# Sixteen more tokens by row gather, routing by four heads, and a second-table sum that grows in the tile of the normalized tokens

## The chip, the cores and the metric

The kernel runs on one core of a Trainium2 chip. The metric is the device time of one execution in microseconds (us), lower is better; differences of over about 0.3% can be told from no change.

## The reference

A decoder block for 512 tokens of width 2048, all in float32: an RMS norm, one input projection to 10240 columns, a gated short convolution and a stick-breaking attention side by side, their gated merge, an output projection with the residual, and then an expert network (PEER). The change lies in the last part:

```python
def peer_ffn(x, wq, subkeys, u_table, v_table):
    q = jnp.einsum("btd,dq->btq", x, wq).reshape(b, t, PEER_HEADS, 2, PEER_HALF)
    scores = jnp.einsum("bthsc,snc->bthsn", q, subkeys)
    top_s, top_i = lax.top_k(scores, PEER_TOPK)
    cand_s = top_s[..., 0, :, None] + top_s[..., 1, None, :]
    cand_i = top_i[..., 0, :, None] * PEER_KEYS + top_i[..., 1, None, :]
    sel_s, sel_pos = lax.top_k(cand_s.reshape(...), PEER_TOPK)
    sel_i = jnp.take_along_axis(cand_i, sel_pos, axis=-1)
    gate = jax.nn.softmax(sel_s, axis=-1)
    # of each token: 8 heads x 16 experts, out of 16384
    hidden = jnp.einsum("td,thkd->thk", xb, u_table[idx])
    act = jax.nn.gelu(hidden, approximate=False) * gate
    return jnp.einsum("thk,thkd->td", act, v_table[idx])
```

The result is added to the residual and normalized once more (norm_final).

## The kernel before, in words

**Two ways to the experts.** The first `G0` tokens (128 + 64 = 192) fetch the rows of the two tables that they chose, by indirect DMA from the POOL queue. The other `ND` = 320 tokens go through all 16384 experts on TensorE ("dense"): `up` multiplies them with every block of 128 rows of the first table, `gates` builds planes that hold each token's gate or zero, and `products` multiplies the gated activations with the second table. The gathers run in the background of everything that comes after the routing of the first tokens.

**Products.** Each weight half tile (128 x 1024) is loaded by SP, rounded to fp32r by ScalarE (`whi`, L133), and VectorE takes the remainder (`wlo`, L134). Each product is then three matmuls (`mm3`, L163: lines L164, L165, L166) of 128 x 128 weights by the columns of the tokens: 256 columns in the mixer's and the queries' projections, 320 (all `ND` tokens) in `up` (tile `pj`) and in `products` (tile `z`). Up and down have 2048 products each.

**Routing** (`route`, L549) works on a tile of 128 tokens, all 8 heads at once: top 16 of each of 16 score groups, the 64 possible sums of two lists, their top 16, the positions' decoding (small operations on [128, 8, 16]), one-hot sums for the expert numbers, the gates. The order of this side work is written out: `background` (L956) is called once for each half weight tile and lets the routing go on for a share of its own cost marks (`yield 2.0` and so on); `pump` (L906) lets the gather go on by RATE rounds for each unit (a whole weight tile). In the dense part the rate is worked out so that all rounds are done some ten units before the end.

**Gather** (`gather_tile`, L676): one round fetches one row of 2048 for each of 128 partitions (1 MB, L685) into one of four buffers `row`. For the first table VectorE multiplies it with the normalized tokens `gx` and sums (L696); for the second it adds the row times its activation to `acc` (L703), which is itself one of the four `row` buffers, loaded with the residual at its start. Tokens 0 to 127 take 128 rounds of each table. The next 64 tokens lie twice on the partitions, each copy with half of the slots, so 64 rounds of each table; `finish` adds the two halves and the norm and the store follow (`finish_rows`, L722; its sum of squares by `rms_scale`, L189, goes through two PSUM tiles `z`).

**The end.** Before the last chunk's `down` the rest of the gather is let run ("last", L919). The residual of the dense tokens is loaded into the same `row` buffers (L882). As each of eight pairs of column blocks is done, TensorE transposes it back in three groups of tokens (`tr`, L843), VectorE adds it to the residual (L845), ScalarE takes squares (L847), VectorE multiplies the gain (L848). The last three rows are scaled and stored.

The program is put in order by a scheduler with a simulated time line, engine by engine; each engine runs its list in that order.

Of the kernel before, what the change touches and what calls it, by code (L numbers as in the profile page):

```python
# [25 lines left out]
H = 8  # L26
# [5 lines left out]
NG2 = 64  # L32
# [48 lines left out]
def block_kernel(ctx, tc, a, out, dbg=None):  # L81
# [107 lines left out]
    def rms_scale(pool, x):  # L189
        ss = pool.tile([P, 2], F32, name="ss", bufs=2)  # L190
        for c in range(2):
            junk = ztile()
            nc.scalar.activation(junk, x[:, c * 1024:c * 1024 + 1024], AF.Square, accum_out=ss[:, c:c + 1])  # L193
        return rms_inv(ss)

    def rms_inv(ss):
        nc.vector.tensor_tensor(ss[:, 0:1], ss[:, 0:1], ss[:, 1:2], OP.add)
        nc.scalar.activation(ss[:, 0:1], ss[:, 0:1], AF.Sqrt, scale=1.0 / D, bias=epst)
# [3 lines left out]
    def turn(x2, k, pin):  # L202
        """Two 128-column blocks of the pair of row tiles, transposed: [128, 2, 256]."""
# [9 lines left out]
    def load_x(h):  # L213
        """Transposed tokens of one half times the norm's gains, split; 1 / rms of each token to inv."""
# [206 lines left out]
    def suffix(pool, z, sp, seg, nj, W):  # L421
        """z minus the sums of sp over the keys from each key to the end."""
# [22 lines left out]
    def outproj(pool, h, m, box):  # L445
        """Output projection and residual of 256 tokens."""
# [38 lines left out]
    def chain(pool, h, box, nhi, nlo, c0):  # L485
        """Normalized, transposed and split tokens of one half from column c0; tokens 0.. to xn2d."""
# [35 lines left out]
    def queries(pool, h, st, nhi, nlo, c0):  # L522
        """Product-key scores of 256 tokens, queued for the top 16 of each group."""
# [25 lines left out]
    def route(pool, tile_no, st):  # L549
        """Product-key routing of one 128-token tile: expert halves and gate of each slot."""  # L550
        ls = pool.tile([P, 2, 8, 2, 16], F32, name="ls", bufs=1)
        tv, ti = ls[:, 0], ls[:, 1].bitcast(U32)
        for _ in range(8):
            while not st["topk"][tile_no]:
                yield "wait"
            for _ in range(2):
                src, g = st["topk"][tile_no].pop(0)
                tmp = pool.tile([P, P], F32, name="ttmp", bufs=2)
                top16(tmp, src, tv[:, g // 2, g % 2], ti[:, g // 2, g % 2])
            yield 2.0  # L560
        tif = pool.tile([P, 8, 2, 16], F32, name="tif", bufs=1)
# [166 lines left out]
    def gather(routes):  # L728
# [6 lines left out]
        if not NG2:  # L735
            return
# [351 lines left out]
```

## Time and profile before

| | us |
|---|---|
| median of 3 runs | 3630.6 |
| the three runs | 3629.32, 3630.6, 3640.37 |
| profiled execution, span | 3629.1 |

The profiled execution is known by its span, first instruction to last, 3629.1 us; it is 1.5 us under the median of the runs. TensorE is busy 3535.7 us of it (97%), VectorE 2833.4 (78%), ScalarE 1621.6 (45%), GpSimd 644.8 (18%). A busy TensorE is not yet TensorE at its peak: its matmuls overlap, so the count of matmuls in a stretch says more than the busy share.

### The profile page before, as it was taken

The numbers are of one execution on the slowest core, as the hardware profiler recorded it, in microseconds if no ns is written. First come the engines' busy times: TensorE is split into PE (matmuls) and PEld (weight loads), VectorE is DVE, ScalarE is ACT, GpSimd is POOL, SyncE is SP. The second block draws the span as 40 slices with busy tenths as digits, with TensorE's granted clock in tenths as the row PEclk, the third lists the DMA queues.
The fourth block names the chain that finished last, engine by engine and source line by source line (L and its number), as shares of the span: only waits on it lengthen the run. The fifth ranks groups of instructions, "written<-read, shape, count | busy, mean of one in ns | idle before, by whom it ended". The sixth has DMA issues, their size and how long they took to land.

```text
span 3629.1 us, 63343 instructions
## 1 busy us (share of the span) xinstructions
PE 3535.7 (97%) x25347; PEld 3420.6 (94%) x25347; DVE 2833.4 (78%) x4022; ACT 1621.6 (45%) x2277; POOL 644.8 (18%) x520
## 2 busy tenths in 40 slices
PE   9999999999999999889999999999999999999998
PEld 8999999798888999779999999999999999999997
DVE  6555557558988888788999886888887888888885
ACT  5444445445545543554337773333333333333334
POOL 0000000000234222012121111221122322322220
PEclk9999999999999999999999999999999999999998
DMA  5556666663788899899889889899988988889884
GB/s 194 170 176 219 214 216 216 198 193 127 267 306 332 335 344 356 313 331 344 295 324 334 309 317 364 326 358 337 341 328 327 358 328 336 325 338 349 326 319 150
DMA packets 297815, 1056.10 MB, mean 291 GB/s; under 512 B 36464, under 2 KB 109296, under 8 KB 243568
## 3 DMA queue, kind: packets, MB, share of 16 engines
q1 hardware_dynamic: 242224, 649.38, 51.3%
q0 software_dynamic: 55296, 402.68, 28.9%
q8 instruction: 199, 3.26, 0.3%
q14 instruction: 96, 0.79, 0.1%
HBM read 999.98 MB, written 51.38 MB: 290 GB/s over the span
## 4 chain that ended last, share of the span: by engine, by line
PE 73%; DVE 3%; DMA 2%; issue 2%; ACT 1%; POOL 0%; SPq 0%; DVEq 0%; ACTq 0%; POOLq 0%
PE pj L166 13%; PE pj L164 13%; PE pj L165 13%; PE z L164 9%; PE z L165 9%; PE z L166 9%; PE pj L668 2%; DVE wlo L134 1%; PE z L434 1%; PE tr L416 1%; DVE row L696 1%; DMA wraw<-in_w_mix 1%; DMA row<-in_u,idx 1%; PE z L397 0%; DMA gt<-gd 0%
## 5 line engine op out<-in xcount | busy, mean ns | idle before, releaser
L133 ACT ACTIVATE whi<-wraw 128x1024 fp32r<-128x1024 f32 x827 | 874.2, 1059 | 1229.3 <-PE pj L165 726.4
L134 DVE TENSOR_TENSOR wlo<-wraw,whi 128x1024 fp32r<-128x1024 f32 x827 | 1009.2, 1224 | 415.3 <-ACT whi L133 409.5
L166 PE MATMUL pj<-xhi,wlo 128*128 128x256 f32 x2560 | 719.7, 282 | 11.3 <-DVE wlo L134 11.1
L164 PE MATMUL pj<-xhi,whi 128*128 128x256 f32 x2560 | 721.6, 282 | 6.7 <-ACT whi L133 4.7
L165 PE MATMUL pj<-xlo,whi 128*128 128x256 f32 x2560 | 720.5, 282 | 0.0
L164 PE MATMUL pj<-dxhi,whi 128*128 128x320 f32 (+1 forms) x2304 | 710.0, 308 | 2.8 <-ACT whi L133 2.6
L166 PE MATMUL pj<-dxhi,wlo 128*128 128x320 f32 (+1 forms) x2304 | 704.1, 307 | 4.5 <-DVE wlo L134 4.5
L165 PE MATMUL pj<-dxlo,whi 128*128 128x320 f32 (+1 forms) x2304 | 705.8, 307 | 0.0
L164 PE MATMUL z<-ahi,whi 128*128 128x320 f32 x2048 | 631.0, 309 | 4.0 <-ACT z L193 2.9
L165 PE MATMUL z<-alo,whi 128*128 128x320 f32 x2048 | 631.5, 309 | 2.4 <-DVE alo L134 2.4
L166 PE MATMUL z<-ahi,wlo 128*128 128x320 f32 x2048 | 629.6, 309 | 1.8 <-DVE wlo L134 1.8
L166 PEld LDWEIGHTS pj<-xhi,wlo 128*128 128x128 f32 x2560 | 480.0, 188 | 21.5 <-DVE wlo L134 16.1
L164 PEld LDWEIGHTS pj<-xhi,whi 128*128 128x128 f32 x2560 | 481.7, 188 | 12.6 <-ACT whi L133 6.1
L165 PEld LDWEIGHTS pj<-xlo,whi 128*128 128x128 f32 x2560 | 481.4, 188 | 6.7 <-issue 5.3
L685 POOL DMA_INDIRECT row<-in_v,idx x192 | 286.7, 1493 | 1063.8 <-DVE row L703 448.9
L703 DVE SCALAR_TENSOR_TENSOR row<-row,gact 128x2048 f32<-128x2048 f32 x192 | 450.5, 2346 | 19.3 <-DMA row<-in_v,idx 19.3
L696 DVE SCALAR_TENSOR_TENSOR row<-row,gx 128x2048 f32<-128x2048 f32 x192 | 438.4, 2287 | 26.0 <-DMA row<-in_u,idx 25.0
L685 POOL DMA_INDIRECT row<-in_u,idx x192 | 290.8, 1515 | 857.8 <-DVE row L696 213.0
L166 PEld LDWEIGHTS pj<-dxhi,wlo 128*128 128x128 f32 x2304 | 433.3, 188 | 5.6 <-DVE wlo L134 5.6
L164 PEld LDWEIGHTS pj<-dxhi,whi 128*128 128x128 f32 x2304 | 434.5, 189 | 3.2 <-ACT whi L133 2.9
L165 PEld LDWEIGHTS pj<-dxlo,whi 128*128 128x128 f32 x2304 | 434.2, 188 | 0.0
L133 ACT ACTIVATE whi<-spare 128x1024 fp32r<-128x1024 f32 x197 | 208.8, 1060 | 414.8 <-PE z L165 263.8
(232 smaller groups left out, 5019.3 us busy)
## 6 DMA issues: line engine op xcount, KB each, us to landing
wraw<-in_w_in SPq DMA_DIRECT2D x320, 512.0 KB
wraw<-in_uT SPq DMA_DIRECT2D x187, 512.0 KB
wraw<-in_vT SPq DMA_DIRECT2D x128, 512.0 KB
spare<-in_vT SPq DMA_DIRECT2D x128, 512.0 KB
spare<-in_uT SPq DMA_DIRECT2D x69, 512.0 KB
wraw<-in_w_mix SPq DMA_DIRECT2D x64, 512.0 KB
wraw<-in_w_out SPq DMA_DIRECT2D x64, 512.0 KB
wraw<-in_wq SPq DMA_DIRECT2D x64, 512.0 KB
```

The lines of the kernel that those rows point to most:

```text
L133: nc.scalar.activation(hi, src, AF.Copy)
L134: nc.vector.tensor_tensor(lo, src, hi.bitcast(F32), OP.subtract)
L164: nc.tensor.matmul(acc, shi, mhi, start=first, stop=False)
L165: nc.tensor.matmul(acc, shi, mlo, start=False, stop=False)
L166: pe_last[0] = nc.tensor.matmul(acc, slo, mhi, start=False, stop=last)
L416: nc.tensor.matmul(yps[hs, q0:], kv[j // 2][1][:, j % 2, hs], e[:, seg(j)], start=j == 0, stop=j == last, skip_group_check=True)
L434: nc.tensor.matmul(z[:, c], stat.bitcast(F32), src[:, c], start=False, stop=True, skip_group_check=True)
L668: behind(nc.tensor.matmul(gp[:, t * P:t * P + P], oh[:, t, 0], oh[:, t, 1], start=True, stop=True))
L685: ins = nc.gpsimd.indirect_dma_start(out=g, out_offset=None, in_=tab, in_offset=bass.IndirectOffsetOnAxis(ap=idx[0:np_, s:s + 1], axis=0))
L696: pin(nc.vector.scalar_tensor_tensor(g, g, 1.0, gx, OP.mult, OP.mult, accum_out=hid[:, s:s + 1]))
L703: pin(nc.vector.scalar_tensor_tensor(acc[0:np_], g, act[:, s:s + 1], acc[0:np_], OP.mult, OP.add))
```

## The change

The gathered tokens become 128 + 64 + 16 = 208 (`NG2` = 80), the dense ones 304. The gather goes through a list of segments; the 16 tokens lie eight times on the partitions and take 16 rounds of each table, and their partial sums are added in three halvings. `route` handles four heads at a time, for tiles 0, 1, 0, 1; each half writes its own list of indices, and the gather of tile 0 starts as soon as the first half's list stands. The sum over the second table grows in `gx`, the tile of the normalized tokens, and no longer in a `row`; the residual is added at the end. `rms_scale` squares in eight pieces of 256 into an SBUF tile `junk`.

```diff
-NG2 = 64
+SEGS = ((0, 0, 128), (1, 0, 64), (1, 64, 16))
+NG2 = 80
...
     def rms_scale(pool, x):
-        ss = pool.tile([P, 2], F32, name="ss", bufs=2)
-        for c in range(2):
-            junk = ztile()
-            nc.scalar.activation(junk, x[:, c * 1024:c * 1024 + 1024], AF.Square, accum_out=ss[:, c:c + 1])
-        return rms_inv(ss)
+        ss = pool.tile([P, 8], F32, name="ss", bufs=2)
+        for c in range(8):
+            junk = pool.tile([P, 256], F32, name="junk", bufs=1)
+            nc.scalar.activation(junk, x[:, c * 256:c * 256 + 256], AF.Square, accum_out=ss[:, c:c + 1])
+        nc.vector.tensor_reduce(ss[:, 0:1], ss, AX.X, OP.add)
+        return rms_root(ss)
...
-    def route(pool, tile_no, st):
+    def route(pool, tile_no, hh, st):
...
-        for _ in range(8):
+        for _ in range(4):
             while not st["topk"][tile_no]:
                 yield "wait"
...
         for s, ab in enumerate((fa, fb)):
-            for h in range(0, H, 4):
-                oh = spare().rearrange("p (h s k) -> p h s k", h=4, s=16)
...
+            oh = spare().rearrange("p (h s k) -> p h s k", h=4, s=16)
...
+        if tile_no * P < G0:
+            ef = pool.tile([P, 64], F32, name="fa", bufs=1)
+            nc.vector.scalar_tensor_tensor(ef, flat[:, 0, fs], 128.0, flat[:, 1, fs], OP.mult, OP.add)
+            idx = late[1].tile([P, 64], I32, name=f"idx_{hh}", bufs=2)
+            nc.vector.tensor_copy(idx, ef)
+            st["idx"][tile_no].append(idx)
...
         def consume(tab, s, g):
-            nonlocal acc
...
             if s == 0:
                 nc.scalar.activation(act[:, :nslot], hid[:, :nslot], AF.Gelu)
                 nc.vector.tensor_tensor(act[:, :nslot], act[:, :nslot], gate[0:np_], OP.mult)
-                acc = row()
-                load_acc(acc)
-            pin(nc.vector.scalar_tensor_tensor(acc[0:np_], g, act[:, s:s + 1], acc[0:np_], OP.mult, OP.add))
+                pin(nc.vector.tensor_scalar(gx, g, act[:, 0:1], None, OP.mult))
+                return
+            pin(nc.vector.scalar_tensor_tensor(g if s == nslot - 1 else gx, g, act[:, s:s + 1], gx, OP.mult, OP.add))
...
+        for tile_no, p0, n in SEGS:
+            R = P // n
...
+            def finish(t):
+                m = P // 2
+                while m >= n:
+                    o = row()
+                    nc.sync.dma_start(o[0:m], t[m:2 * m])
+                    nc.vector.tensor_tensor(t[0:m], t[0:m], o[0:m], OP.add)
+                    m //= 2
+                o = row()
+                nc.sync.dma_start(o[0:n], x2d[rows])
+                nc.vector.tensor_tensor(t[0:n], t[0:n], o[0:n], OP.add)
+                finish_rows(t, rows, final_gain())
...
     def routing(h):
-        for tt in range(2):
-            yield from route(rts[0], 2 * h + tt, st)
+        for hh in range(2):
+            for tt in range(2):
+                yield from route(rts[0], 2 * h + tt, hh, st)
...
-        due = min(due, 0.0) + (SIDE_A0 if not st["routes"][0] else SIDE_A if unit < GATES_AT else SIDE_G)
+        due = min(due, 0.0) + (SIDE_A0 if not st["idx"][0] else SIDE_A if unit < GATES_AT else SIDE_G)
...
-        if st["routes"][0] and what != "half":
+        if st["idx"][0] and what != "half":
```

How the lists of the engines move is seen at three places.

The POOL queue from the last attention pair of the second half on, before (`in_u` and `in_v` are the tables, `idx` the lists of rows):

```order
L408 AFFINE_SELECT row<-row 128x2x128
L685 DMA row<-in_u,idx 128x2048 x76
L685 DMA row<-in_v,idx 128x2048 x128
L685 DMA row<-in_u,idx_29423 128x2048 x64
L685 DMA row<-in_v,idx_29423 128x2048 x64
```

The same place of the POOL queue now:

```order
L414 AFFINE_SELECT row<-row 128x2x128
L699 DMA row<-in_u,idx_10978 128x2048 x61
L699 DMA row<-in_v,idx_9188 128x2048 x64
L699 DMA row<-in_v,idx_10978 128x2048 x64
L699 DMA row<-in_u,idx_28199 128x2048 x64
L699 DMA row<-in_v,idx_28199 128x2048 x64
L699 DMA row<-in_u,idx_35474 128x2048 x16
L699 DMA row<-in_v,idx_35474 128x2048 x16
```

Behind the last attention pair 332 fetches stood before, 349 stand there now; of the first table's first 128, 52 stood ahead of that place before and 67 do now.

VectorE's list from the next to last accumulation `dacc` of the last chunk on, before (`z` is the product's tile, `tr` the transposes', `row_37134`, `row_37137` and `row_37140` the three groups of dense tokens):

```order
L838 TENSOR_TENSOR dacc_23877<-z_37641,dacc_23877 128x640
L845 TENSOR_TENSOR row_37140<-tr_37468,row_37140 128x256
L848 TENSOR_TENSOR row_37140<-row_37140,row_37132 128x256
L845 TENSOR_TENSOR row_37134<-tr_37537,row_37134 64x256
L848 TENSOR_TENSOR row_37134<-row_37134,row_37132 64x256
L838 TENSOR_TENSOR dacc_23877<-z_37724,dacc_23877 128x640
L845 TENSOR_TENSOR row_37137<-tr_37544,row_37137 128x256
L845 TENSOR_TENSOR row_37140<-tr_37551,row_37140 128x256
```

The same place now (`row_37167` holds the sums of the last 16 gathered tokens, `row_37413`, `row_37416` and `row_37419` the three groups of dense tokens):

```order
L852 TENSOR_TENSOR dacc_24020<-z_37920,dacc_24020 128x608
L862 TENSOR_TENSOR row_37413<-row_37413,row_37411 48x256
L196 TENSOR_REDUCE ss_37389<-ss_37389 128x1
L205 RECIPROCAL ss_37389<-ss_37389 128x1
L739 SCALAR_TENSOR_TENSOR row_37167<-row_37167,ss_37389,row_37387 128x2048
L852 TENSOR_TENSOR dacc_24020<-z_38003,dacc_24020 128x608
L859 TENSOR_TENSOR row_37416<-tr_37491,row_37416 128x256
L862 TENSOR_TENSOR row_37416<-row_37416,row_37411 128x256
L859 TENSOR_TENSOR row_37419<-tr_37498,row_37419 128x256
```

Before, 12 of the 24 groups (eight pairs of blocks by three groups of tokens) were added ahead of the last accumulation and 12 behind it; now one stands ahead and 23 behind.

SP's list at the end, now (the x2d rows are the residual of the dense tokens, the 16 x 2048 one that of the last gathered tokens):

```order
L150 DMA wraw<-in_vT 128x1024
L767 DMA row<-row 64x2048
L150 DMA spare<-in_vT 128x1024
L767 DMA row<-row 32x2048
L767 DMA row<-row 16x2048
L771 DMA row<-x2d 16x2048
L733 DMA row<-in_norm_final 128x2048 x2
L896 DMA row<-x2d 48x2048
L740 DMA out<-row 16x2048
L896 DMA row<-x2d 128x2048 x2
L911 DMA out<-row 48x1024 x2
```

Two of the three residual loads stand behind the store of the last gathered tokens and behind the last weights; before, the store was followed by these two loads too, but six half weight tiles still came after the first and four after the second.

## Rows read from the trace of the kernel before

**Rows 1.** The page's busy times, and its slices of PE, VectorE and DMA.
```profile
PE 3535.7 (97%) x25347; PEld 3420.6 (94%) x25347; DVE 2833.4 (78%) x4022; ACT 1621.6 (45%) x2277; POOL 644.8 (18%) x520
...
DMA  5556666663788899899889889899988988889884
```
**Rows 2.** Busy us of each engine by stretch, matmul counts in brackets, granted clock, DMA share, GB/s.
```profile
400.00:500.00 100.00, 100.00 (x851) 100.00 (x850) 57.63 (x70) 42.54 (x52) 0.00 (x0) 1.00 0.72 224
...
2900.00:3000.00 100.00, 100.00 (x684) 100.00 (x683) 81.86 (x85) 35.61 (x45) 25.01 (x17) 1.00 0.87 332
```
**Rows 3.** Instructions by line and form, whole span: busy us, mean ns, idle before.
```profile
L164 PE MATMUL z<-ahi,whi 128*128 128x320 f32 x2048 | 631.0, 309 | 4.0 <-ACT z L193 2.9 <-DVE dacc L838 0.7
...
L668 PE MATMUL pj<-spare 128*128 128x128 f32 x640 | 86.2, 275 | 0.6 <-DVE spare L651 0.6
```
**Rows 4.** The same view, VectorE.
```profile
L703 DVE SCALAR_TENSOR_TENSOR row<-row,gact 128x2048 f32<-128x2048 f32 x192 | 450.5, 2346 | 19.3 <-DMA row<-in_v,idx 19.3
L696 DVE SCALAR_TENSOR_TENSOR row<-row,gx 128x2048 f32<-128x2048 f32 x192 | 438.4, 2287 | 26.0 <-DMA row<-in_u,idx 25.0 <-DVE wlo L134 1.0
...
L547 DVE FIND_INDEX8 ls<-ls,ttmp 128x8 uint32<-128x128 f32 x64 | 18.1, 288 | 0.0
...
L547 DVE FIND_INDEX8 pos<-sv,ttmp 128x8 uint32<-128x64 f32 x32 | 6.7, 220 | 0.0
```
**Rows 5.** Stretches as in rows 2: routing beside the mixer, and beside the first dense products.
```profile
800.00:1200.00 400.00, 384.70 (x2758) 335.64 (x2757) 345.32 (x704) 214.44 (x250) 112.45 (x107) 1.00 0.72 258
...
1700.00:1890.00 190.00, 187.18 (x1291) 186.62 (x1290) 183.72 (x490) 73.74 (x89) 34.99 (x25) 0.99 0.88 321
```
**Rows 6.** Stretches as in rows 2, where the DMA engines are fullest.
```profile
1300.00:1400.00 100.00, 98.63 (x830) 97.80 (x829) 80.57 (x86) 41.75 (x52) 20.89 (x15) 1.00 0.95 349
...
2200.00:2700.00 500.00, 490.94 (x3314) 487.30 (x3313) 421.32 (x401) 173.88 (x207) 99.86 (x71) 1.00 0.92 342
2700.00:3500.00 800.00, 797.13 (x5433) 796.44 (x5432) 653.15 (x595) 285.04 (x348) 213.58 (x130) 1.00 0.89 336
```
**Rows 7.** The same, two short stretches and the fullest of 100 us.
```profile
2360.00:2380.00 20.00, 19.88 (x136) 19.64 (x135) 16.33 (x14) 6.57 (x7) 5.03 (x3) 1.00 1.05 396
1840.00:1860.00 20.00, 20.00 (x139) 20.00 (x138) 19.11 (x42) 7.14 (x9) 6.12 (x4) 1.00 1.02 412
...
2300.00:2400.00 100.00, 99.76 (x679) 99.28 (x679) 86.53 (x84) 35.26 (x40) 22.74 (x14) 1.00 0.93 354
```
**Rows 8.** Time line, the finish of the last gathered tokens: start us, us, engine, line.
```profile
3534.30 2.35 DVE L703 SCALAR_TENSOR_TENSOR row<-row,gact 128x2048 f32<-128x2048 f32 x1
...
3536.68 0.48 SPq L757 DMA_DIRECT2D row<-row  x1
...
3542.09 2.28 DVE L758 TENSOR_TENSOR row<-row 64x2048 f32<-64x2048 f32 x1
...
3552.65 0.52 SPq L726 DMA_DIRECT2D out<-row  x1
```
**Rows 9.** Time line, from the last accumulation to the end.
```profile
3605.22 0.82 DVE L838 TENSOR_TENSOR dacc<-z,dacc 128x640 f32<-128x640 f32 x1 [0.29 <-PE z L166]
3605.96 0.41 DVE L845 TENSOR_TENSOR row<-tr,row 128x256 f32<-128x256 f32 x1
...
3614.30 0.42 DVE L845 TENSOR_TENSOR row<-tr,row 128x256 f32<-128x256 f32 x1
...
3615.35 0.42 DVE L848 TENSOR_TENSOR row<-row 128x256 f32<-128x256 f32 x1 [0.63 <-ACT hd L847]
3615.69 0.41 DVE L845 TENSOR_TENSOR row<-tr,row 64x256 f32<-64x256 f32 x1
...
3618.85 0.41 DVE L845 TENSOR_TENSOR row<-tr,row 128x256 f32<-128x256 f32 x1
```

More of the change, by code (lines that the diff above doesn't have):

```diff
@@ L620, in route @@
-        idx = None
-        if tile_no * P < G0:
-            ef = pool.tile([P, P], F32, name="fa", bufs=1)
-            nc.vector.scalar_tensor_tensor(ef, flat[:, 0], 128.0, flat[:, 1], OP.mult, OP.add)
-            idx = late[1].tile([P, P], I32, name="idx", bufs=2)
-            nc.vector.tensor_copy(idx, ef)
-            if tile_no == 0:
-                st["gate"] = late[1].tile([P, P], F32, name="gate", bufs=1)
-                nc.vector.tensor_copy(st["gate"], flat[:, 2])
-        if dbg:
-            nc.sync.dma_start(dbg["eg"][tile_no], flat)
@@ L728, in gather @@
     def gather(routes):
-        idx = routes[0][0]
-        yield from gather_tile(
-            late[1], P, P, idx, st["gate"],
-            lambda t: nc.sync.dma_start(t, xn2d[0:P]),
-            lambda t: nc.sync.dma_start(t, x2d[0:P]),
-            lambda t: finish_rows(t, slice(0, P), final_gain()))
-        if not NG2:
-            return
-        S = P // (P // NG2)
-        idx, eg = routes[1]
-        idx2 = late[1].tile([P, S], I32, name="idx2")
-        gate2 = late[1].tile([P, S], F32, name="gate2")
@@ L741, in gather, with load_x @@
-        for r in range(P // NG2):
-            ps_, ss = slice(r * NG2, r * NG2 + NG2), slice(r * S, r * S + S)
-            nc.sync.dma_start(idx2[ps_], idx[0:NG2, ss])
-            nc.sync.dma_start(gate2[ps_], eg[0:NG2, 2, ss])
-        def load_x(t):
-            for r in range(P // NG2):
-                nc.sync.dma_start(t[r * NG2:r * NG2 + NG2], xn2d[P:G0])
-        def load_acc(t):
-            nc.vector.memset(t, 0.0)
-            nc.sync.dma_start(t[0:NG2], x2d[P:G0])
-        def finish(t):
-            for r in range(1, P // NG2):
+        for tile_no, p0, n in SEGS:
+            R = P // n
+            rows = slice(tile_no * P + p0, tile_no * P + p0 + n)
+            idx, gate = st["idx"][tile_no], st["gate"]
+            if R > 1:
+                src, eg = routes[tile_no]
+                idx = [late[1].tile([P, n], I32, name=f"idx{n}")]
+                gate = late[1].tile([P, n], F32, name=f"gate{n}")
+                for r in range(R):
+                    ps_, ss = slice(r * n, r * n + n), slice(r * n, r * n + n)
+                    c = r * n % 64
+                    nc.sync.dma_start(idx[0][ps_], src[r * n // 64][p0:p0 + n, c:c + n])
+                    nc.sync.dma_start(gate[ps_], eg[p0:p0 + n, 2, ss])
+            def load_x(t):
+                for r in range(R):
+                    nc.sync.dma_start(t[r * n:r * n + n], xn2d[rows])
+            def finish(t):
[5 more added lines that the diff above has]
+                    m //= 2
@@ L756, in finish @@
                 o = row()
-                nc.sync.dma_start(o[0:NG2], t[r * NG2:r * NG2 + NG2])
-                nc.vector.tensor_tensor(t[0:NG2], t[0:NG2], o[0:NG2], OP.add)
-            finish_rows(t, slice(P, G0), final_gain())
-        yield from gather_tile(late[1], P // NG2 * NG2, S, idx2, gate2, load_x, load_acc, finish)
+                nc.sync.dma_start(o[0:n], x2d[rows])
+                nc.vector.tensor_tensor(t[0:n], t[0:n], o[0:n], OP.add)
+                finish_rows(t, rows, final_gain())
@@ L763, in dense @@
+            yield from gather_tile(late[1], P, n, idx, gate, load_x, finish)
     def dense(pool, st):
@@ L897, in dense @@
                 nc.sync.dma_start(out[G0 + c:G0 + c + n, half * 1024:half * 1024 + 1024], xs)
-    st = {"routes": [None] * 4}
+    st = {"routes": [None] * 4, "eg": [None] * 4, "idx": [[] for _ in range(4)]}
     credit = 0.0
@@ L903, in block_kernel @@
     pumped = [0]
-    rounds = 2 * P + (2 * (P // (P // NG2)) if NG2 else 0)
+    rounds = sum(2 * n for _, _, n in SEGS)
     def pump(rate):
```

79 lines of the change are left out of this document (47 added, 32 removed).

## The prediction

> **What bounds the kernel now.** I read the page's busy times first [rows 1]: TensorE is busy 97% of the span and VectorE 78%. A busy TensorE says little, so I counted matmuls in stretches [rows 2]. With 256 columns 851 end in 100 us, 117.5 ns each; with 320 columns 684, 146.2 ns each. Both are 0.457 to 0.459 ns per column, so a product costs what its columns cost, and in the second of these stretches TensorE never waits although VectorE is busy 82% and the DMA engines 87%. The reader is to see two things more. VectorE is nearly full in two places [rows 5]: 345.3 of 400 us from 800 to 1200 us, where the first routing meets the mixer and TensorE loses 15.3 us, and 183.7 of 190 us from 1700 to 1890 us, where TensorE loses only 2.8. And the DMA engines are nearly full from 2200 us on [rows 6], at 342 and 336 GB/s. So TensorE is the bound, with little room under it on two sides.
>
> **The products.** Sixteen dense tokens go. Up and down have 2048 products of three matmuls each, 2 x 3 x 2048 = 12288 matmuls, in six groups like the first of [rows 3]. At 0.457 ns per column, 304 columns take 138.9 ns instead of 146.2: 12288 x 7.3 ns = **-89.7 us**. By the chord between the two rates (28.7 ns for 64 columns) it is 7.2 ns, or 88 us; the two bound this term closely. The Trainium skill ("TensorE: Matmul & The Clock Gate", Back-to-back issue gap) gives a matmul at the full clock its columns at 2.4 GHz and 2.5 ns more, so only 6.7 ns for 16 columns. By that rule the term would be -82 us; but it also gives 135.8 ns for 320 columns, where rows 2 show 146.2, so the trace decides.
>
> **Small gains.** One gate plane block of 20 goes, 5% of L668's 86.2 us of overlapping matmuls [rows 3]: between 0 and -4, taken as -2. The squares of a finished row leave PSUM, so a product no longer waits for its tile `z`: the 2.9 us behind ACT L193 [rows 3]: -3. The sum in `gx` frees one of four `row` buffers while the second table is fetched; VectorE waited for those rows 19.3 us in all, TensorE not: 0.
>
> **More rounds.** 32 more rounds, 16 of each table, at 2.29 (and a short read of the sum) and 2.35 us [rows 4], are 75 us of VectorE. Halving the heads doubles some 27 small operations per tile. The nearest price of a halving is FIND_INDEX8, 0.288 us for 128 elements and 0.220 for 64 [rows 4]: two halves cost 0.15 us more than the whole, so 27 x 4 x 0.15 = 16 us. From 16 columns fewer in `dacc`, `hd` and the splits some 10 us come back. VectorE does about 80 us more, of some 790 us that it had free; where it falls decides.
>
> *Mixer.* The POOL list puts 15 more fetches ahead of the last attention pair, because the gather starts on half the heads. That is 15 x 2.37 = 36 us of VectorE, mostly between 800 and 1200 us, where it had 54.7 us free [rows 5], only some 6 of them between 900 and 1000. Nothing hides all of it: the bounds are 0 and 36 us. Close to the row where VectorE was full and TensorE lost 1.5% [rows 5], 400 us would lose 6; some hundred us will be oversubscribed, so I take **+10**.
>
> *Second routing, 1700 to 2000 us.* VectorE is full, and TensorE's gain there (5% of 190 us, 9.5 us) needs VectorE to keep pace; half the added routing work (8 us) falls here too. Bounds 0 and 18; I take **+10**. What is late next is `wlo`.
>
> *DMA.* From 2200 to 2700 us 171 MB move, from 2700 to 3500 us 269 MB [rows 6]. The list puts about 3 and 10 more rounds of 1.05 MB there; hidden activations and gate planes shrink by about 1.5 MB in all. Both stretches would shrink by 5%, to 475 and 760 us, and would need 365 and 366 GB/s, at a DMA share of 0.97 to 0.98. Stretches of 20 us reached 396 and 412 GB/s with TensorE at work [rows 7], but the fullest 100 us only 354. TensorE lost 1.4 of 100 us at a share of 0.95 [rows 6]. Taking that for the 1235 us gives 17; weights are loaded up to seven half tiles ahead, which hides bursts. Bounds 0 and 41 (at 354 GB/s, 452 MB take 1276 us); I take **+14**.
>
> **The end.** Before, 12 of the 24 groups of transposed output are behind the last accumulation, now 23. A group takes 1.39 us (3614.30 to 3615.69), because the gain's multiply waits for ScalarE's square [rows 9]; the earlier 11 steps took 12.9 us in all. 22 steps x 1.39 = 30.6, so +17.7. The residual of two groups can be loaded only after the last 16 tokens are finished. That finish took 18.4 us from the start of the last sum to the store's issue, with one exchange of halves (3536.68 to 3544.37, 7.7 us) [rows 8]; now there are three, and a further add of 2.3 us, so about 36 us, and squares in eight pieces. The last sum stands some 260 matmuls (36 us) ahead of the end, so the loads leave at about the end of the products and take as long as the exchange's DMA, some 5 us: +6, bounds 0 and 13. Ten groups fewer among the products give 4 back. Sum **+20**, bounds 14 and 31. SP's queue holds no weights behind these loads, so nobody else waits.
>
> **Others.** A third finish, eight more table loads of ScalarE (45% busy [rows 1]) and 16 small DMAs of indices and gates on SP: +2, beside seven half tiles of weights already loaded; without that cover perhaps 10.
>
> **Sum.** -89.7 - 2 - 3 + 10 + 10 + 14 + 20 + 2 = -38.7 us. The profiled execution has 3629.1 us, 1.5 under the median; 3629.1 - 38.7 = **3590 us**.
>
> **The rivals.**
>
> *The DMA engines become the bound (0.2).* Demand of 365 GB/s over a thousand us has no precedent [rows 6, 7]; for it also speaks that the share is 0.89 to 0.92 already. If 354 GB/s is what lasts, the two stretches take 1276 us instead of 1235 + 14: 27 us above the forecast, **3617 us**. Against it speak the 396 and 412 GB/s. The Trainium skill ("DMA: Bandwidth & Descriptors", Specifications) gives about 358 GB/s as what HBM can give one core; by that rule 452 MB would take 1262 us and the time would be some 3603 us. Rows 7 stand above this figure for 20 us each, and no row shows it for a millisecond.
>
> *All of it hides (0.1).* VectorE and the DMA engines keep up, and the end costs its lower bound: 3629.1 - 94.7 + 14 + 2 = **3550 us**. For it speaks that TensorE lost almost nothing from 2700 to 3500 us [rows 6].
>
> *VectorE waits for the gathered rows, and the products for VectorE (0.07).* VectorE's list is fixed, so a late row holds back the splits behind it. It waited 45 us in 384 rounds, 0.12 us each [rows 4]. From 2200 us on there will be about 219 rounds. With VectorE busy 88% (81.6% now [rows 6], times the faster pace and more rounds), a round of 5.5 us leaves 0.66 us of room. This decides from 0.9 us of waiting per round: at 1.0 us, 219 x 0.34 = 74 us are lost, **3664 us**, slower than before.
>
> *The products don't become cheaper (0.03).* If something else than columns sets the 146 ns, 89.7 us don't come and the costs stay: about **3680 us**. The 117.5 ns of 256 columns [rows 2] speak against it.
>
> **How the numbers follow.** The forecast has the remaining 0.6. Its own bounds go from 3560 to 3624 with two or three costs at an end; 3617 lies inside, the two slow rivals and the most of the 3550 us one outside, so the range is **3558 to 3624**. Differences under 0.3%, 11 us, can't be told from none. Faster by more: 0.6 x 0.97 + 0.2 x 0.7 + 0.1 = 0.82; slower by more: 0.10 from the last two; the same: 0.08.
>
> **What would show it.** Right: some 720 matmuls in 100 us between 2900 and 3300 us; 32 more indirect fetches; VectorE at 86 to 89% there and above 90% between 850 and 1100 us; some 44 us from the last accumulation to the end, in steps of 1.39 us behind a gap of about 6. The DMA rival would show as `whi` waiting for `wraw` and `spare`, and a share of 1.0 at 350 to 360 GB/s; the VectorE rival as VectorE idle behind `row` at L707 and L714, and TensorE behind `wlo`. The forecast is wrong if fewer than 700 matmuls end in those 100 us, or if the end costs less than 30 us.

## The result, and the profile after

The changed kernel takes 3669.7 us (median of 4; 3662.2 to 3678.2), the kernel before 3635.5 us in the same comparison: a ratio of 1.0102, 95% interval 1.0087 to 1.0117. It is 1.0% slower, where 1% faster was forecast. The profiled execution has a span of 3660.1 us, 31.0 more than before. Where they lie, by the starts of three matmuls: the first one of the dense products by count (in the changed kernel two of them, at 1744.1 us, trade places with the last of 256 columns), the first one into `z`, and the first one of the last product:

| us | before | after | difference | forecast |
|---|---|---|---|---|
| up to the first dense product | 1716.4 | 1747.6 | +31.2 | +10 |
| dense: the first 1024 products of `up` (second routing beside them) | 521.6 | 509.9 | -11.7 | -12 |
| dense: the other 3072 products | 1366.6 | 1354.7 | -11.9 | -58 |
| behind the last product | 24.5 | 47.9 | +23.4 | +20 |

In the forecast column the 89.7 us of the products are shared out by their number: 22.4 to the second line, with +10 for routing; 67.3 to the third, with -2, -3 and +14 for the DMA engines; the +2 for others is left out. So two lines came as forecast and two did not: VectorE ahead of the dense part cost three times as much, and of the dense part 46 us are missing.

First the page's busy times [rows 1], then stretches as in rows 2, of the kernel after:

```profile
PE 3483.1 (95%) x25315; PEld 3353.3 (92%) x25315; DVE 2902.5 (79%) x4164; ACT 1633.6 (45%) x2311; POOL 735.4 (20%) x552
```
```profile
2700.00:3500.00 800.00, 777.20 (x5491) 773.30 (x5490) 668.87 (x616) 292.65 (x363) 231.15 (x139) 0.99 0.91 347
2900.00:3000.00 100.00, 96.08 (x683) 95.33 (x682) 84.29 (x87) 34.99 (x44) 31.77 (x18) 1.00 0.90 353
800.00:1200.00 400.00, 372.67 (x2650) 327.42 (x2649) 358.63 (x723) 204.84 (x241) 126.44 (x118) 0.99 0.77 286
1700.00:1890.00 190.00, 187.98 (x1398) 186.99 (x1397) 184.44 (x477) 79.94 (x97) 43.00 (x28) 1.00 0.90 327
```

From 2900 to 3000 us 683 matmuls start, as many as before [rows 2], where 720 were expected; under 700 was to show the forecast wrong. TensorE now stands still for 22.8 us of the 800, and for 2.9 before [rows 6]. From 1700 to 1890 us there are 1398 instead of 1291 [rows 5], but about half of these 107 show only that the changed kernel is still at products of 256 columns until 1747.6 us. That the cheaper products came through here is read from the second line of the table.

TensorE's busy time in the third line's stretch, before and after, leaves gaps of 8.2 and 44.0 us:

```profile
2238.00:3605.00 1367.00, 1358.80 (x9243) 1354.49 (x9243) 1123.31 (x1052) 489.16 (x607) 313.33 (x201) 1.00 0.88 327
```
```profile
2257.00:3612.00 1355.00, 1311.00 (x9221) 1300.33 (x9221) 1144.55 (x1066) 494.22 (x627) 381.61 (x215) 0.99 0.91 342
```

What TensorE waits for in it, before and after: us in total, times, longest.

```profile
PE z L166 <- DVE wlo L134: 1.8, 1, 1.8
```
```profile
PE z L168 <- DVE wlo L136: 29.0, 19, 4.0
PE z L166 <- ACT whi L135: 8.8, 6, 5.1
PE pj L168 <- DVE wlo L136: 2.9, 3, 1.7
```

And VectorE there, before and after:

```profile
DVE wlo L134 <- ACT whi L133: 147.5, 120, 2.6
DVE dacc L838 <- PE z L166: 62.0, 56, 2.5
```
```profile
DVE wlo L136 <- ACT whi L135: 83.7, 73, 6.1
DVE dacc L852 <- PE z L168: 79.5, 64, 4.7
DVE hd L788 <- ACT hd L812: 14.6, 16, 1.6
```

TensorE waits for `wlo`, and VectorE, which makes `wlo`, waits for TensorE. Before, VectorE waited for TensorE too, but hardly any of it came back to the products. VectorE's time line at the longest of these waits (start, duration, line, operation, and the idle time before it):

```profile
3018.26 1.28 DVE L712 TENSOR_SCALAR gx<-row,gact 128x2048 f32<-128x2048 f32 x1
3024.24 0.79 DVE L852 TENSOR_TENSOR dacc<-z,dacc 128x608 f32<-128x608 f32 x1 [4.71 <-PE z L168]
3024.95 2.34 DVE L714 SCALAR_TENSOR_TENSOR gx<-row,gact,gx 128x2048 f32<-128x2048 f32 x1
3027.21 1.22 DVE L136 TENSOR_TENSOR wlo<-spare,whi 128x1024 fp32r<-128x1024 f32 x1
3028.35 1.22 DVE L136 TENSOR_TENSOR wlo<-wraw,whi 128x1024 fp32r<-128x1024 f32 x1
```

VectorE is idle for 4.71 us because the next entry of its list, the accumulation L852, needs the end of a running product. The two splits for the next product stand behind it, and behind a sum of the gather too, although ScalarE had rounded their halves by 3018.5 and 3021.8 us. When they come at last, TensorE has stood still for 4.00 us (3024.5 to 3028.5). In VectorE's list 15 accumulations of the down products have no split of weights between them and the one before; in the kernel before there were 6.

The end, VectorE's time line [rows 9]:

```profile
3612.88 0.79 DVE L852 TENSOR_TENSOR dacc<-z,dacc 128x608 f32<-128x608 f32 x1 [0.80 <-PE z L168]
3617.88 0.42 DVE L859 TENSOR_TENSOR row<-tr,row 128x256 f32<-128x256 f32 x1 [4.20 <-DMA row<-x2d]
3618.88 0.42 DVE L862 TENSOR_TENSOR row<-row 128x256 f32<-128x256 f32 x1 [0.58 <-ACT hd L861]
3620.50 0.42 DVE L859 TENSOR_TENSOR row<-tr,row 128x256 f32<-128x256 f32 x1 [1.20 <-DMA row<-x2d]
...
3621.84 0.41 DVE L859 TENSOR_TENSOR row<-tr,row 48x256 f32<-48x256 f32 x1
...
3648.24 0.41 DVE L859 TENSOR_TENSOR row<-tr,row 128x256 f32<-128x256 f32 x1
```

From the start of the accumulation to the first group 5.0 us pass, for the late load; from 3621.84 to 3648.24 us there are 19 steps of 1.39 us. This is the end as it was predicted.

### The profile page after: what moved, and what is told of

It reads as the page before. It is cut to its first block, busy times and chain, and to the rows that moved or that the text cites. A ratio compares the mean times of both kernels' runs of the same rounds, so it can differ in the third digit from the quotient of the medians.

```text
span 3660.1 us, 63542 instructions
## 1 busy us (share of the span) xinstructions
PE 3483.1 (95%) x25315; PEld 3353.3 (92%) x25315; DVE 2902.5 (79%) x4164; ACT 1633.6 (45%) x2311; POOL 735.4 (20%) x552
## 3 DMA queue, kind: packets, MB, share of 16 engines
q0 software_dynamic: 59904, 436.23, 30.7%
## 5 line engine op out<-in xcount | busy, mean ns | idle before, releaser
L166 PE MATMUL pj<-dxhi,whi 128*128 128x304 f32 (+1 forms) x2304 | 698.3, 303 | 6.9 <-ACT whi L135 6.6
L168 PE MATMUL pj<-dxhi,wlo 128*128 128x304 f32 (+1 forms) x2304 | 690.8, 302 | 10.7 <-DVE wlo L136 10.5
L167 PE MATMUL pj<-dxlo,whi 128*128 128x304 f32 (+1 forms) x2304 | 694.1, 302 | 0.0
L168 PE MATMUL z<-ahi,wlo 128*128 128x304 f32 x2048 | 621.6, 306 | 29.1 <-DVE wlo L136 29.0
L166 PE MATMUL z<-ahi,whi 128*128 128x304 f32 x2048 | 622.5, 305 | 11.0 <-ACT whi L135 8.8
L167 PE MATMUL z<-alo,whi 128*128 128x304 f32 x2048 | 622.9, 305 | 0.0
L699 POOL DMA_INDIRECT row<-in_v,idx x208 | 358.7, 1725 | 1005.1 <-DVE gx L714 204.8
L707 DVE SCALAR_TENSOR_TENSOR row<-row,gx 128x2048 f32<-128x2048 f32 x208 | 474.3, 2285 | 50.7 <-DMA row<-in_u,idx 49.4
L168 PEld LDWEIGHTS pj<-xhi,wlo 128*128 128x128 f32 x2560 | 483.5, 189 | 29.4 <-DVE wlo L136 25.8
L714 DVE SCALAR_TENSOR_TENSOR gx<-row,gact,gx 128x2048 f32<-128x2048 f32 x202 | 473.5, 2344 | 12.3 <-DMA row<-in_v,idx 12.0
L168 PEld LDWEIGHTS z<-ahi,wlo 128*128 128x128 f32 x2048 | 388.5, 190 | 34.6 <-DVE wlo L136 34.6
```

The costliest lines, as they stand in the source:

```text
L166: nc.tensor.matmul(acc, shi, mhi, start=first, stop=False)
L167: nc.tensor.matmul(acc, shi, mlo, start=False, stop=False)
L168: pe_last[0] = nc.tensor.matmul(acc, slo, mhi, start=False, stop=last)
L699: ins = nc.gpsimd.indirect_dma_start(out=g, out_offset=None, in_=tab, in_offset=bass.IndirectOffsetOnAxis(ap=idx[s // w][0:np_, s % w:s % ...
L707: pin(nc.vector.scalar_tensor_tensor(g, g, 1.0, gx, OP.mult, OP.mult, accum_out=hid[:, s:s + 1]))
L714: pin(nc.vector.scalar_tensor_tensor(g if s == nslot - 1 else gx, g, act[:, s:s + 1], gx, OP.mult, OP.add))
```

## The experiments

Times are medians; "before" is the kernel before in the same comparisons (3633.8 to 3636.4 us). The stretches of each run in the table's sense stand where they decide.

**Splits ahead of the accumulation.** `products` loads and splits the next down product's two half tiles ahead of `dacc`, and `dacc` is queued behind the second split.

```diff
+            for dp, c in nxt:
+                wnext[dp, c] = whalf(a["vT"][ch, dp, c])
             for zt, dp in zip(zs, dps):
...
                     mark(nc.vector.tensor_tensor(av, zv, av, OP.add))
+                    if nxt:
+                        tc.add_manual_dep(anchors[-1].ins, wlast[0].ins.name, ..., reason="split first")
```

> The changed kernel, with the two half tiles of weights of the next down product split ahead of the accumulation of the present one in VectorE's list; no work is added or taken away. Theory (TensorE waits in the dense part because an accumulation, which waits for the end of a product, stands ahead of the splits that the next product needs): the 29 us that z L168 waits for wlo fall under 8, the dense part gets 20 to 30 us shorter, about 3645 us (3638 to 3652). Rivals, that VectorE has too much work there or that the DMA engines are late: no order helps, within 5 us of 3669.7 us.

3632.1 us, 0.9995 of before (0.9986 to 1.0005): 37.6 us back, more than expected. Its waits and its stretches:

```profile
PE z L169 <- ACT whi L135: 8.1, 5, 5.1
PE pj L171 <- DVE wlo L136: 6.9, 4, 1.7
PE z L171 <- DVE wlo L136: 3.8, 5, 1.5
```
```profile
2700.00:3500.00 800.00, 792.98 (x5652) 791.75 (x5652) 691.94 (x634) 302.32 (x377) 253.27 (x144) 1.00 0.94 360
2900.00:3000.00 100.00, 100.00 (x717) 100.00 (x716) 86.64 (x91) 37.45 (x47) 31.07 (x19) 1.00 0.93 365
```

With the same work, 717 matmuls start in those 100 us, and TensorE never waits while VectorE is busy 87% and 365 GB/s move. The wait for `wlo` in `z` falls from 29.0 to 3.8 us, the stretch from 1354.7 to 1322.3. Neither too much work on VectorE nor late transfers can explain the 32.4 us that come back there; the order of the lists does.

**The same order in the kernel before.** The same edit.

> The kernel before the change, with the same new order as the run that splits first: the two half tiles of the next down product ahead of the accumulation in VectorE's list. Theory (the order costs only where the list had gone wrong, which is in the changed kernel): TensorE's gaps in the dense part of the kernel before are 16 us in all, so it gains at most 8 us: 3626 to 3636 us. Rival (the order is a gain for any of these kernels, and the change has nothing to do with it): 20 us or more, below 3615 us.

3633.2 us (1.0001; 0.9992 to 1.0011), as the theory had it: nothing to mend there.

**304 columns without the third segment.**

```diff
-SEGS = ((0, 0, 128), (1, 0, 64), (1, 64, 16))
+SEGS = ((0, 0, 128), (1, 0, 64))
```

> The changed kernel without the third segment: 16 of the 512 tokens get no second half and aren't stored, so 32 rounds, a finish and their transfers are gone, while the products keep 304 columns; the order of VectorE's list is left to itself, as in the changed kernel. It asks whether 304 columns alone spoil the dense part. Theory (the list goes wrong with the pace of the rounds): the list now has 8 accumulations with no split since the one before them, where the changed kernel has 15 and the kernel before 6, so TensorE's waits for wlo in the products fall from 29 us to about 12; the stretch ahead of the dense part stays at 1018 us; the end is 12 groups shorter, about 30 us; 3610 to 3632 us. Rival (304 columns alone): the waits stay at 25 us or more and the time is 3640 us or above.

3589.0 us, less than either expected; the 16 tokens are left out, so the time is of use for this question only. The wait for `wlo` in `z` is 3.0 us, and the 3072 products take 1299.8 us, 66.8 less than before: the whole 67.3 that their columns should give. So the columns spoil nothing; 32 more rounds and a third finish do. That they do it by way of the lists rests on the run that splits first, for the 32.4 us that it gave back. The stretch ahead of the dense part is as long as in the changed kernel (to 1751.9 us) and the end is 30.3 us.

**Two segments, 320 columns.** As above, and in `rms_scale` the old lines.

```diff
-NG2 = 80
+NG2 = 64
...
-            junk = pool.tile([P, 256], F32, name="junk", bufs=1)
+            junk = ztile()
```

> The third segment goes (192 gathered tokens, 320 columns, 384 rounds as before) and the squares pass through PSUM again; what stays of the change is the routing by four heads, the earlier start of the gather and the sum in gx. Theory (a full VectorE ahead of the dense part, an order of VectorE's list that puts accumulations ahead of splits in it, and a longer end): the stretch from 727 us to the first dense product stays about 31 us longer than before (1020 us, between 1005 and 1025), the dense products cost 146 ns each again, the end is as before (about 25 us); 3655 to 3668 us as the median. Rival, the transfers of 32 more rounds: they are gone, so the time returns to that of before, 3630 to 3640 us.

3655.5 us (1.0062; 1.0045 to 1.0079): 28 us are lost ahead of the dense part (to 1744.3 us) with no further segment, and the end is 26.4. The theory holds.

**A later start.**

```diff
-        due = min(due, 0.0) + (SIDE_A0 if not st["idx"][0] else SIDE_A if unit < GATES_AT else SIDE_G)
+        due = min(due, 0.0) + (SIDE_A0 if not st["routes"][0] else SIDE_A if unit < GATES_AT else SIDE_G)
...
-        if st["idx"][0] and what != "half":
+        if st["routes"][0] and what != "half":
```

The first line goes with the second: the routing's faster pace (`SIDE_A0`) lasts again until a whole tile is routed.

> The changed kernel, but the gather starts when a whole tile of 128 tokens is routed, as before the change; routing stays in two passes of four heads. Theory (the 15 rounds that start earlier fall where VectorE has no room): of the 31 us that the stretch ahead of the dense part lost, 15 to 25 come back; the rounds that move into the dense part cost some of it again, so 3645 to 3662 us. Rival, the many small operations of routing by four heads: the stretch stays within 6 us of 1020 us, and the time at 3665 to 3675 us.

The stretch ahead of the dense part ends at 1706.8 us, 40.8 earlier than in the changed kernel and 9.6 earlier than before, with the same routing by four heads, so the smaller operations are not its loss. VectorE begins 110 rounds ahead of the dense part here, 134 in the changed kernel and 118 before. Whether the early start costs by itself or by the rounds that it adds, this run can't tell; the run with the rounds spread can (below). (In one execution each of the changed kernel and of seven runs with the same code for this part the stretch ends between 1745 and 1754 us, so a few us either way mean nothing.) But the time is 3699.4 us, a miss: the 24 rounds that moved come too late. Busy times of this stretch in the kernel before, the changed one, and this run:

```profile
727.00:1716.00 989.00, 948.20 (x7029) 873.90 (x7029) 803.98 (x1356) 482.98 (x623) 219.28 (x182) 0.99 0.81 295
```
```profile
727.00:1747.00 1020.00, 953.31 (x6991) 876.52 (x6991) 839.88 (x1451) 481.08 (x610) 238.27 (x200) 0.98 0.82 303
```
```profile
727.00:1707.00 980.00, 934.93 (x6998) 867.86 (x6997) 786.86 (x1402) 469.65 (x601) 204.08 (x175) 0.98 0.79 289
```

VectorE does 804.0, 839.9 and 786.9 us of work; 53.0 us more between the last two make the stretch 40 us longer, 0.75 us for each. Of what this run loses again, 22.7 us are in the 3072 products (1377.4 us) and 42.2 at the end (VectorE's time line; the last product starts at 3601.5 us):

```profile
3610.61 2.35 DVE L714 SCALAR_TENSOR_TENSOR row<-row,gact,gx 128x2048 f32<-128x2048 f32 x1 [0.71 <-DMA row<-in_v,idx]
...
3638.49 0.42 DVE L859 TENSOR_TENSOR row<-tr,row 48x256 f32<-48x256 f32 x1 [5.31 <-DMA row<-x2d]
```

The last sum now stands behind the last product, and all 24 groups wait for its finish: 90.1 us.

**An earlier last round.**

```diff
-DRAIN = 10
+DRAIN = 24
```

> The changed kernel, with the rounds paced so that the last segment ends some 14 steps of the dense loop (100 us) earlier (DRAIN 24 for 10); the rounds stand 6% closer together. Theory (the rows of dense tokens are loaded behind the last finish, so all 23 groups of the end are multiplied by the gain after the products): the end falls from 47.8 us to about 31 us or less, some 17 us, and the closer pace costs up to 6 back; 3650 to 3662 us. Rival, that the end is set by the chain of transposed groups whatever the loads do: within 4 us of 3669.7 us, plus what the pace costs.

The end falls to 35.2 us, but the time rises to 3683.4, a miss: the 3072 products take 1380.5 us, 25.8 more than in the changed kernel, and TensorE's wait for `wlo` in `z` grows from 29.0 to 39.8 us, with 21 accumulations in the list without a split before them instead of 15:

```profile
PE z L168 <- DVE wlo L136: 39.8, 30, 4.0
```

**Squares through `z` again**, as before the change, beside splits first.

```diff
-        for c in range(8):
-            junk = pool.tile([P, 256], F32, name="junk", bufs=1)
+        for c in range(2):
+            junk = ztile()
```

> The run that splits first, with the squares of a finished row in two pieces through a PSUM tile z again, as before the change. Theory (a finish whose squares stand in no product's way is put late in the lists): with z the products behind it wait for the finish, so the lists put the last finish about 78 products earlier and 12 instead of one of the 24 groups of the end among the products; the end falls from 44 us to about 28, and TensorE waits some 3 us for z at each of three finishes but loses the 8 us behind ScalarE's eight squares: 3612 to 3622 us. Rival (the squares are worth the 3 us of the wait they took away, and the end is late for its three exchanges): 3632 to 3640 us.

3660.0 us, 28 slower than with `junk` and outside both expectations. The end is 24.2 us, better than expected; the wait was mispriced by far:

```profile
PE z L169 <- ACT z L198: 51.2, 3, 26.7
```

With three exchanges ahead of the squares, a product that has to follow them waits up to 26.7 us.

**The sum in a `row` again**, beside splits first.

```diff
+                acc = row()
-                pin(nc.vector.tensor_scalar(gx, g, act[:, 0:1], None, OP.mult))
+                pin(nc.vector.tensor_scalar(acc, g, act[:, 0:1], None, OP.mult))
```

> The run that splits first, with the second table's sum in one of the four row buffers again. The prediction priced the freed buffer at nothing. Theory now (fetches wait for a free row, so three buffers hold back 416 rounds): the lists put the last sums behind the last product, where the run that splits first has them about 100 products ahead of it; the end grows from 44 us to 80 or more, 3665 to 3690 us. Rival (the buffer is worth nothing, as predicted): within 6 us of 3632 us.

3692.1 us: the end is 99.8. At this pace three buffers don't carry 416 rounds; the last sums follow the last product, and wait for their rows:

```profile
3602.50 2.35 DVE L721 SCALAR_TENSOR_TENSOR row<-row,gact 128x2048 f32<-128x2048 f32 x1 [1.90 <-DMA row<-in_v,idx]
```

**The groups of the end.** First the gains move into the final scaling; then the transposes take turns in three tiles.

```diff
-                        nc.vector.tensor_tensor(xs, xs, gfin[0][0:n, dp * 256:dp * 256 + 256], OP.mult)
...
+                nc.vector.scalar_tensor_tensor(xs, xs, rn, gfin[0][0:n, half * 1024:half * 1024 + 1024], OP.mult, OP.mult)
```
```diff
-                        tr = trtile()
+                        tr = accum()
```

> The run that splits first, with the last norm's gains multiplied in the final scaling of the dense rows (four products of 1024 columns) and not group by group. Theory (the 23 groups of the end cost 1.39 us each because the multiply by the gains waits for ScalarE's square and holds up the next group): a group falls to some 0.6 us, 22 x 0.8 = 17 us, less 3 for the longer scaling; the end falls from 44 to about 30 us, 3618 us (3612 to 3624). Rival (the transposes or ScalarE set the 1.39 us): within 5 us of 3632 us.

3631.3 us, a miss: the square was not what set the pace. TensorE's time line shows what did:

```profile
3606.03 0.69 PE L864 MATMUL tr<-ident,dacc 128*128 128x128 f32 x2 [0.51 <-DVE row L866]
3607.23 0.69 PE L864 MATMUL tr<-ident,dacc 128*128 128x128 f32 x2 [0.52 <-DVE row L866]
```

A step is 1.2 us: 0.69 of transposes and 0.51 in which VectorE empties the one tile `tr`.

> The run with the gains last, and the transposes of the end now take turns in the three PSUM tiles pj instead of the one tile tr. With the gains gone from the groups a group still took 1.2 us, since TensorE waits for VectorE to empty tr and VectorE for TensorE to fill it again. Theory (that hand-over is what is left): a group falls to 0.7 us, 22 x 0.5 = 11 us; the end falls from 42 to about 31 us, 3620 us (3614 to 3627). Rival (the end hangs on the late loads of the rows, not on the groups): within 4 us of 3631 us.

3613.6 us (0.9938; 0.9913 to 0.9963); the end is 24.6 us.

> The kernel before the change, with splits first, the gains in the final scaling and the transposes in the three tiles pj: what the later runs added to the changed kernel, without the change. Theory (these edits matter where 23 groups stand behind the products; before the change 12 do, in an end of 24.4 us): the end falls by 12 x 0.7 = 8 us at most; 3626 us (3622 to 3632), so that most of the distance between the kernel before and the best run belongs to the change itself. Rival (the end's new form is the whole gain): below 3615 us.

3626.2 us (0.998; 0.997 to 0.9989). The kernel before gains 7.6 us by the same edits and splits first.

**The rounds spread.** On top of splits first and both edits of the end:

```diff
-RATE_A = 1.35
+RATE_A = 1.0
-DRAIN = 10
+DRAIN = 16
-RV = 0.9
+RV = 1.05
```

> The run with three tiles for the transposes, with the early start kept but the rounds spread: 1.0 round per step of the mixer instead of 1.35, 1.05 instead of 0.9 of the even pace in the first half of the dense loop, and the last round six steps earlier (DRAIN 16); 60 rounds are in VectorE's list ahead of product 2880 instead of 75. Theory (a round ahead of the dense part costs 41 us / 24 rounds = 1.7 us, one in the dense part nearly nothing while the splits go first): the stretch ahead of the dense part falls from 1020 to about 995 us, the dense part grows by at most 8, the end shrinks by 5; 3598 us (3588 to 3610). Rival (VectorE has no room in the dense part either): the dense part takes back what the stretch ahead of it gains, 3615 to 3625 us.

**3594.5 us, 0.9882 of before (0.9857 to 0.9908)**, the best version; 31.7 us under the kernel before with the same end. The kernel before was not tried at other paces, so how much of the 31.7 the new pace would give there too stays open. The stretch ahead of the dense part ends at 1716.8 us, as before the change, with as much work of VectorE in it (803.5 us up to 1716). Of the three constants only `RATE_A` acts ahead of the dense part. The gather starts as early as in the changed kernel (first fetch at 829 us, 828 there, 917 before), the heads are routed in fours, and VectorE begins 119 rounds ahead of the dense part, where the changed kernel begins 134 and the kernel before 118. So it was the number of rounds there that cost the 31 us, and neither the early start by itself nor the routing by four heads. Two stretches:

```profile
2231.00:3578.00 1347.00, 1312.25 (x9243) 1298.46 (x9242) 1181.46 (x1093) 498.79 (x651) 375.56 (x229) 0.99 0.95 358
2700.00:3500.00 800.00, 794.37 (x5643) 789.13 (x5643) 704.12 (x642) 303.06 (x378) 252.65 (x148) 1.00 0.96 366
```

Three other paces, each with the same order and end; their edits against the run with the rounds spread are, in turn (the second against the first of them):

```diff
-RATE_A = 1.0
-RATE_O = 0.8
+RATE_A = 1.35
+RATE_O = 1.1
...
-        due = min(due, 0.0) + (SIDE_A0 if not st["idx"][0] else SIDE_A if unit < GATES_AT else SIDE_G)
+        due = min(due, 0.0) + (SIDE_A0 if not st["routes"][0] else SIDE_A if unit < GATES_AT else SIDE_G)
...
-        if st["idx"][0] and what != "half":
+        if st["routes"][0] and what != "half":
```
```diff
-RATE_A2 = 0.85
-RATE_O = 1.1
-RV = 1.05
+RATE_A2 = 1.0
+RATE_O = 1.2
+RV = 1.1
```
```diff
-RATE_O = 0.8
-RV = 1.05
+RATE_O = 1.2
+RV = 0.95
```

> The run with three tiles for the transposes, the start of the gather on whole routed tiles (51 rounds ahead of product 2880), 1.1 rounds per step at the end of the mixer and in the second output projection instead of 0.8, 1.05 of the even pace in the first half of the dense loop, DRAIN 16. Theory: the stretch ahead of the dense part falls to some 982 us, the dense part grows by 5 to 12 us from some 20 more rounds, the end is 28 to 32 us; 3585 us (3575 to 3598). Rival (a full VectorE in the dense part): 3605 us or more.

> As the run before it, with more rounds just ahead of the dense part (1.0 and 1.2 rounds per step instead of 0.85 and 1.1; 128 instead of 117 rounds by product 3840) and 1.1 of the even pace. It asks where a round is cheapest. If VectorE has room in the second output projection (40 us idle in 155 there), as the theory has it, the time stays within 6 us of the run before it; if a round costs 1.7 us there as in the mixer, 11 rounds make it 19 us longer.

> As the run with the rounds spread, but with 1.2 rounds per step instead of 0.8 at the end of the mixer and in the second output projection (128 instead of 120 rounds by product 3840), and 0.95 instead of 1.05 of the even pace in the first half of the dense loop, where that run lost some 20 us between products 4800 and 5760 with VectorE over 90% busy. Theory (a round costs only where VectorE is full): the dense part gets 8 to 15 us shorter and the stretch ahead of it at most 5 longer, 3587 us (3580 to 3594). Rival (a round costs the same anywhere): within 4 us of 3594.5 us.

They took 3604.7, 3598.8 and 3610.4 us. The first and the last miss: the later start kept the first stretch at 1714.7 instead of some 1709, and the 3072 products took 1355.4 us (1346.8 with the rounds spread); the last run lost 12 us ahead of the dense part, with 9 more rounds there, and won 3 behind. The second came as expected, within 6 us of the first. Where a round is cheapest stays open: these runs move rounds and the scheduler's lists at once.

## Why the prediction was wrong

**Products, -89.7.** Right in price: 717 matmuls in 100 us are 139.5 ns each, 138.9 was said, and without the third segment 66.8 of 67.3 us came.

**Mixer, +10.** This step failed: +31.2 us came of it. It counted 36 us of VectorE correctly (839.9 - 804.0), but took most of them as hidden, by the 1.5% that TensorE lost in a stretch where VectorE was full already. That row says nothing of what more work costs. Here 16 rounds were added to a mixer that had 54.7 us free in 400 and already lost 15.3 [rows 5]. By the busy times above, TensorE's gaps in it grew from 40.8 to 66.7 us, and some 20 of these 26 us are waits for `wlo` (727 to 1750 us, before and after):

```profile
PE pj L166 <- DVE wlo L134: 12.1, 17, 1.7
```
```profile
PE pj L168 <- DVE wlo L136: 28.8, 24, 4.3
...
PE z L167 <- DVE wlo L136: 3.9, 4, 2.1
```

The place was wrong too: counted by products, the changed kernel is 10.5 us late where the kernel before stands at 1200 us, and 31 us late at the first dense product, so two thirds of the loss lie behind the 400 us that the step looked at. The later start and the spread rounds show the cause.

**Second routing, +10.** Right: 22.4 us expected from columns, 11.7 got. With the same routing and 320 columns (two segments) the stretch takes 523.5 us, only 1.9 more than before. So it is the gain that a full VectorE withholds here, rather than the added routing work; no run tests that alone.

**DMA, +14, and the DMA rival.** Nothing of it shows. No transfer stands among TensorE's waits of the stretch, and ScalarE, which would wait for late weights first, did so for 21 us of the 1355 (11 before); with the splits first 360 GB/s move for 800 us and TensorE stands still for 7. The Trainium skill ("DMA: Bandwidth & Descriptors", Specifications) gives about 358 GB/s for one core; the best run shows that over 1347 us and 366 over 800, so as a ceiling the figure is a little low here.

**What no step had: +55 in the 3072 products** (-11.9 instead of -67.3). I costed VectorE by its room and took its list as given. The scheduler made a new one, and in it accumulations stand ahead of splits. 32.4 of the 55 us come back by order alone. TensorE's gaps grew from 8.2 to 44.0 us in this stretch. Most of the other 20 us is the clock: the trace grants the lower level in six spells of the stretch, 30.7 us in all (none before), which is 15.4 us of full speed. Some 4 us stay unaccounted for. The rival in which products wait for VectorE gave 3664 us and so met the time and the symptom, TensorE behind `wlo`, by luck; its cause is refuted, since VectorE waited for TensorE and not for rows (1.4 us behind a row of the second table in this stretch). It had 0.07, because I asked only whether rows come late.

**Small gains, -3 and 0.** Both edits were priced by the waits they removed from the kernel before. Beside the third segment and splits first they carry far more: 28 us for the squares in `junk`, 60 for the sum in `gx`. The squares have a price too: at the first finish ScalarE's list puts eight of them, a table load and a root ahead of `whi`, and TensorE waits 5.1 us (ScalarE's time line, after):

```profile
2643.97 0.42 ACT L195 ACTIVATE junk<-row 128x256 f32<-128x256 f32 x1
...
2644.50 1.28 ACT L204 ACT_TABLE_LOAD   x1
2645.80 0.29 ACT L204 ACTIVATE ss<-ss,epst 128x1 f32<-128x1 f32 x1
2646.00 1.04 ACT L135 ACTIVATE whi<-spare 128x1024 fp32r<-128x1024 f32 x1
```

**The end, +20.** Right: +23.4, in steps of 1.39 us behind a gap of 5.0. Its reason was half right: the multiply behind the square was in the way, but without it the single tile `tr` holds a step at 1.2 us. The upper bound of 31 leaves out the 4 us given back among the products; with them it is 27.

## What to carry to other kernels

Price background work by what the engine's list puts it in front of, not by that engine's free time: an engine at 84% can stop TensorE if an instruction that waits for TensorE stands ahead of one that TensorE needs. Where an engine is nearly full, as VectorE was in the mixer, take added work at most of its length and not at what is lost there now. Where a scheduler writes the lists, count such inversions in the new list before trusting a sum, and pin the pairs that matter. An edit that looks worth nothing in the old kernel is to be priced under the load that the rest of the change brings.

## What was not expected of the hardware

A gap of TensorE can cost more than its length. After TensorE had stood still for the 4.00 us up to 3028.5, the granted clock was for a time the lower of its two levels (1.2 instead of 2.4 GHz): its means are 0.88 and 0.78. After a gap of 1.74 us (up to 3140.5) it stayed at 1.00, but after another of 1.74 us (up to 2787.6) it fell too. Stretches of 10 us, columns as in rows 2:

```profile
2785.00:2795.00 10.00, 8.26 (x48) 8.02 (x48) 7.63 (x7) 2.12 (x2) 2.79 (x3) 0.83 1.00 377
...
3020.00:3030.00 10.00, 6.00 (x39) 5.76 (x38) 5.76 (x5) 2.12 (x2) 1.71 (x2) 0.88 0.61 233
3030.00:3040.00 10.00, 10.00 (x59) 10.00 (x58) 7.66 (x6) 2.12 (x2) 2.30 (x3) 0.78 0.95 359
3040.00:3050.00 10.00, 10.00 (x74) 10.00 (x73) 8.47 (x7) 3.18 (x3) 1.43 (x1) 1.00 0.70 261
...
3140.00:3150.00 10.00, 7.78 (x54) 7.54 (x55) 8.99 (x7) 2.12 (x2) 3.87 (x2) 1.00 0.64 213
```

A mean clock of 0.88 and 0.78 over 10 us each is 3.4 us of full speed lost, nearly the gap once more: 59 matmuls start from 3030 to 3040 us with TensorE busy throughout, and 74 in the 10 us after.

So the length of a gap does not settle by itself whether the clock falls: in the kernel before it stayed at 1.00 through a gap of 2.87 us (up to 2756.4) and behind it. What settles it stays open here.

```profile
2750.00:2760.00 10.00, 7.13 (x49) 6.87 (x48) 7.93 (x11) 6.95 (x11) 2.77 (x2) 1.00 0.85 312
2756.00:2766.00 10.00, 9.60 (x65) 9.60 (x66) 7.26 (x9) 5.46 (x9) 2.27 (x2) 1.00 0.98 331
```
